# Weights split in one subtraction, and the operands of the last product split one stage earlier

## The chip, the cores and the metric

The kernel runs on one core of a Trainium2 chip. Its time is the device time of one execution in microseconds, the median of several; the profile is one more execution, recorded by the hardware.

## The reference

One encoder block on 512 tokens of width 2048, all in float32:

```
h = rmsnorm(x, norm1_w);  proj = h @ w_in                    # 2048 x 9248
group A, 8 heads: conv + silu, L2 norm, gated delta rule (chunks of 64), forward + backward scans
group B, 8 heads: HGRN2, f = lb + (1 - lb) * sigmoid(f_raw), k = 1 - f, forward + backward scans
x = x + concat(y_a, y_b) @ w_out                             # 2048 x 2048
h2 = rmsnorm(x, norm2_w)
x = x + (silu(h2 @ w_gate) * (h2 @ w_up)) @ w_down           # 2048 x 5632, twice, and 5632 x 2048
out = rmsnorm(x, norm_f_w)
```

## The kernel before

The kernel is written in a tile framework. A planner with a timeline model of the engines lays out the instructions of each engine in a fixed order; a stretch of code under `high_priority(offset=...)` is treated as if it stood that many instructions earlier in the program.

**The products.** Four large products stand one after the other, with the scans between the first and the second: the input projections (36 products of 256 output columns, `projections`, L313), the output product (8, `out_proj`, L866), gate and up (44, `gate_up`, L1028) and the last product, w_down (`down`, L1057). All go through `block_products` (L980), which computes products of 2 x 2 sub-matrices by seven multiplications in place of eight: the weights give seven operands of 128 x 128 (three sub-matrices and four sums), the activations seven of 128 x 256, and `PRODUCTS` (L930) says which meets which. Each operand is split into a high part, rounded to fp32r, and a low part, the rest, and each multiplication is three matmuls: high x high, high x low, low x high. A pair of row tiles is 7 x 3 = 21 matmuls of 256 columns.

**The weights.** `block_weights` (L957) prepares two such pairs at a time, a *block* of 42 matmuls. SyncE's queue loads two pieces of 256 KB into `raw` (three buffers). VectorE makes four sums in `wsum` (two buffers) with three operations (L972 to L974). Then for `raw` (128 x 768) and again for `wsum` (128 x 1024), ScalarE casts to `whi` and VectorE subtracts to `wlo` (L976, L977). `whi` and `wlo` have two buffers each, so a block is prepared while the one before it is multiplied. Where a group of operands has an odd number of pairs, its last block is half as large.

**The activations.** `operands` (L941) makes the seven operands of a pair: three VectorE operations for the sums (`act_sums`, L933), three ScalarE casts, three VectorE subtractions (L954), into slots `oh` and `ol`.

**After a product** `combine` (L1010) turns its four PSUM banks into the result: ScalarE copies one piece into a small tile, then VectorE does five operations (L1019 to L1023).

**Gate, up and the last product.** `gate_up` makes gate and up for 256 columns at a time (22 steps), multiplies them by the token scale (L1050), applies SiLU on ScalarE, multiplies the two (L1054), and stores the 512 KB result to DRAM through ScalarE's queue (L1055). `down` works in four groups of 6, 6, 5 and 5 operands (`DOWN_BLOCKS`, L1026), adding each group's product to an accumulator in SBUF. At the start of a group it loads each result from DRAM (L1070, ScalarE's queue) and splits it with `operands` into one of six slots. The slots of a group are free only when the last products of the group before have used them; the first two products of each group, and the last two of the first three groups, run together, block by block.

**Elsewhere.** In the projections' start (`activations`, L169) the transposed x is scaled by a column per partition on VectorE (L212). The forget gates get `lb + (1 - lb) * s` on VectorE (L389). `hgrn_pair` (L676) makes 1 - f for both directions on VectorE (L688, L689), in the scan stage.

Of the kernel before, what the change touches and what calls it, by code (L numbers as in the profile page):

```python
# [17 lines left out]
P = 128  # L18
T = 512
# [3 lines left out]
DFF = 5632  # L23
# [47 lines left out]
class Block:  # L71
# [97 lines left out]
    def activations(self, tops, acts, tmp):  # L169
# [24 lines left out]
        ops = []  # L194

        def chunk(i):
# [4 lines left out]
            for b in range(2):  # L201
                j = 2 * i + b
                full = tmp.tile([P, 2, T], F32, name=("t", "acc")[b], bufs=2)
                for r in range(2):
                    c = b + 2 * r
                    pt = bank(turn)
                    for t in range(NT):
# [11 lines left out]
                ts = tmp.tile([P, 4, ht], F32, name="comb", bufs=1) if b == 0 else \  # L219
                    tmp.tile([P, 2, T], F32, name="sq", bufs=1).rearrange("p a (b t) -> p (a b) t", b=2)  # L220
# [92 lines left out]
    def projections(self, xops, chunk, tmp):  # L313
# [62 lines left out]
        def post(kind, g, t):  # L376
# [30 lines left out]
        while n < len(self.AHEAD):  # L407
# [9 lines left out]
            for prod, (kind, g) in zip(prods, now):  # L417
                t = tmp.tile([P, 2, 2, ht], F32, name="t", bufs=2)
                self.combine(prod, t, tmp, 1, "comb")
# [256 lines left out]
    def hgrn_pair(self, h0):  # L676
# [11 lines left out]
        nc.vector.tensor_scalar(out=X[:, 0], in0=f[:, 0], scalar1=-1.0, scalar2=1.0, op0=ALU.mult, op1=ALU.add)  # L688
        nc.vector.tensor_scalar(out=X[:, 3], in0=f[:, 1], scalar1=-1.0, scalar2=1.0, op0=ALU.mult, op1=ALU.add)  # L689
# [107 lines left out]
    def mixers(self):  # L797
# [8 lines left out]
        self.wpairs, self.wbufs = 2, (3, 2, 2)  # L806
# [59 lines left out]
    def out_proj(self, late):  # L866
# [4 lines left out]
        def post(p, t):  # L871
# [4 lines left out]
            sq = late.tile([P, 2, T], F32, name="comb", bufs=1)  # L876
# [13 lines left out]
        for ps in ((0, 1), *((p,) for p in range(2, KT // 2))):  # L890
            k = [4 * (p // 2) + p % 2 for p in ps]
            prods = self.block_products([(a["w_out"][0], (i * P, (i + 2) * P)) for i in k], 0, yops, order=self.Y_BLOCKS)
            for p, prod in zip(ps, prods):
                t = late.tile([P, 2, 2, ht], F32, name="t", bufs=2)
                self.combine(prod, t, late, 1, "comb")
# [45 lines left out]
    def operands(self, ab, slot, sums, bufs):  # L941

        nc, ht = self.nc, self.HT
        pool = self.ops[slot // 2]
        h = pool.tile([P, 7, ht], F32R, name=f"oh{slot}")
        l = pool.tile([P, 7, ht], F32R, name=f"ol{slot}")
# [8 lines left out]
        return [h[:, i] for i in range(7)], [l[:, i] for i in range(7)]  # L955

    def block_weights(self, src, col):  # L957
# [6 lines left out]
        raw = cut(self.wst.tile([P, 4 * m, P], F32, name="raw", bufs=bufs[0]), 4)  # L964
        sm = cut(self.wst.tile([P, 4 * m, P], F32, name="wsum", bufs=bufs[1]), 4)
        h = cut(self.wst.tile([P, 7 * m, P], F32R, name="whi", bufs=bufs[2]), 7)
# [209 lines left out]
```

## Time and profile before

| | |
|---|---|
| runs | 2745.14, 2751.14, 2750.34 us; median 2750.34 |
| the profiled execution | 2746.68 us |
| its span | 2744.9 us |
| instructions | 55187 |
| mean granted TensorE clock | 0.963 of 2.4 GHz |
| moved by DMA | 361.89 MB, 132 GB/s on average |
| projections | about 15 to 900 us |
| scans | about 900 to 1140 us |
| output product and its operands | about 1140 to 1390 us |
| gate and up | about 1390 to 2245 us |
| last product | about 2245 to 2745 us |

Times in rows are microseconds from the span's start unless marked ns. PE is TensorE's matmuls, PEld its weight loads, DVE VectorE, ACT ScalarE, POOL GpSimd, SP SyncE; a `q` behind a name is that engine's queue of instructions that are not compute, DMA issues among them. `out<-in` gives tiles by their names in the program: `big` is a PSUM bank, `tsum`, `comb`, `u`, `yt`, `tt` are the tiles of `combine` and `operands`. A busy share of TensorE counts overlapping matmuls once, so the number of its instructions in a stretch says more about its pace. A few matmul records can be missing.

### The profile page before, as it was taken

Reading aid. Unit: us, or ns where it says so; the run is one execution under the profiler, and the core shown is the slowest. Engines: PE = TensorE matmul, PEld = TensorE weight load, DVE = VectorE, ACT = ScalarE, POOL = GpSimd, SP = SyncE. Lnnn points to the kernel's source line nnn. Section 1 sums busy time; section 2 is a strip of 40 time slices with the busy share of each in tenths; the row PEclk is TensorE's granted clock in tenths of the full one; section 3 lists DMA queues with packets and bytes.
Section 4 is the critical chain, followed back from the end, with each engine's and each line's share of the span. In section 5 each row is a group of like instructions: output and inputs, shape, how many; then the busy total and the mean of one; then the engine's idle time right before and its main releaser. Section 6 shows DMA issues by size and latency. Waiting matters only on the chain.

```text
span 2744.9 us, 55187 instructions
## 1 busy us (share of the span) xinstructions
PE 2520.9 (92%) x22511; PEld 2449.8 (89%) x22511; DVE 2506.7 (91%) x3978; ACT 1282.1 (47%) x1777; POOL 296.4 (11%) x148
## 2 busy tenths in 40 slices
PE   6999999888899587889999999999999999899996
PEld 5989999888899476789899999999999999898996
DVE  8999999998999887889998989999899999999996
ACT  6555655445454443444644434344433443444444
POOL 0121112223112554210000000000000000000000
PEclk9999999999999798999999999999999999999998
DMA  6334344556444643546434443434344364434333
GB/s 185 109 101 130 109 132 111 164 156 167 118 143 135 203 134 90 166 145 181 147 114 128 121 124 116 123 119 121 116 124 123 110 200 144 131 106 126 107 93 100
DMA packets 562345, 361.89 MB, mean 132 GB/s; under 512 B 51393, under 2 KB 514683, under 8 KB 562091
## 3 DMA queue, kind: packets, MB, share of 16 engines
q1 hardware_dynamic: 543515, 311.70, 39.6%
q10 hardware_dynamic: 18576, 46.67, 4.8%
q8 instruction: 176, 2.88, 0.4%
q14 instruction: 78, 0.64, 0.1%
HBM read 303.66 MB, written 54.62 MB: 131 GB/s over the span
## 4 chain that ended last, share of the span: by engine, by line
PE 49%; DVE 15%; issue 6%; DMA 4%; ACT 2%; POOL 1%; POOLq 0%; SPq 0%; ACTq 0%; DVEq 0%
PE big L1001 46%; DVE wlo L977 4%; DVE ol L954 1%; DVE wsum L972 1%; DVE wsum L974 1%; DMA L<-d_L 1%; DVE wsum L973 1%; ACT whi L976 1%; POOL acc L473 1%; DVE X L744 1%; DVE X L746 1%; DMA acc<-d_rows 0%; DVE lt L517 0%; DVE tsum L937 0%; PE oT L628 0%
## 5 line engine op out<-in xcount | busy, mean ns | idle before, releaser
L1001 PE MATMUL big<-oh,whi 128*128 128x256 f32 x4144 | 1139.1, 284 | 31.7 <-ACT whi L976 21.1
L1001 PE MATMUL big<-ol,whi 128*128 128x256 f32 x4144 | 1139.5, 282 | 1.8 <-DVE ol L954 1.6
L1001 PE MATMUL big<-oh,wlo 128*128 128x256 f32 x4144 | 1070.6, 283 | 16.8 <-DVE wlo L977 16.4
L1001 PEld LDWEIGHTS big<-oh,whi 128*128 128x128 f32 x4144 | 783.5, 190 | 42.4 <-ACT whi L976 28.8
L976 ACT CAST whi<-raw 128x768 fp32r<-128x768 f32 (+1 forms) x448 | 368.9, 824 | 907.3 <-PE big L1001 649.9
L1001 PEld LDWEIGHTS big<-ol,whi 128*128 128x128 f32 x4144 | 785.6, 190 | 3.3 <-DVE ol L954 2.8
L1001 PEld LDWEIGHTS big<-oh,wlo 128*128 128x128 f32 x4144 | 746.7, 190 | 22.6 <-DVE wlo L977 21.8
L977 DVE TENSOR_TENSOR wlo<-wsum,whi 128x1024 fp32r<-128x1024 f32 (+1 forms) x448 | 542.1, 1210 | 9.5 <-ACT whi L976 9.3
L976 ACT CAST whi<-wsum 128x1024 fp32r<-128x1024 f32 (+1 forms) x448 | 462.0, 1032 | 151.2 <-DVE wsum L974 148.1
L977 DVE TENSOR_TENSOR wlo<-raw,whi 128x768 fp32r<-128x768 f32 (+1 forms) x448 | 432.7, 966 | 85.9 <-ACT whi L976 82.2
L1001 PE MATMUL big<-tp,whi 128*128 128x256 f32 x2304 | 415.0, 286 | 27.9 <-ACT whi L976 17.0
L1001 PEld LDWEIGHTS big<-tp,whi 128*128 128x128 f32 x2304 | 348.5, 193 | 33.6 <-ACT whi L976 19.6
L972 DVE TENSOR_TENSOR wsum<-raw 128x512 f32<-128x512 f32 (+1 forms) x448 | 313.3, 700 | 10.2 <-DMA raw<-in_w_in 3.1
L1001 PE MATMUL big<-tp,wlo 128*128 128x256 f32 x1152 | 293.5, 290 | 21.7 <-DVE wlo L977 21.4
L1001 PE MATMUL big<-xh,whi 128*128 128x256 f32 x864 | 246.1, 289 | 10.4 <-ACT whi L976 7.3
L1001 PE MATMUL big<-xl,whi 128*128 128x256 f32 x864 | 244.8, 287 | 0.0
L1001 PE MATMUL big<-xh,wlo 128*128 128x256 f32 x864 | 229.3, 287 | 4.6 <-DVE wlo L977 4.3
L1001 PEld LDWEIGHTS big<-tp,wlo 128*128 128x128 f32 x1152 | 206.8, 195 | 28.8 <-DVE wlo L977 28.3
L974 DVE TENSOR_TENSOR wsum<-wsum,raw 128x256 f32<-128x256 f32 (+1 forms) x448 | 206.9, 463 | 2.4
L973 DVE TENSOR_TENSOR wsum<-wsum,raw 128x256 f32<-128x256 f32 (+1 forms) x448 | 189.4, 424 | 3.6
L1001 PEld LDWEIGHTS big<-xh,whi 128*128 128x128 f32 x864 | 167.7, 194 | 12.3 <-ACT whi L976 8.4
L1001 PEld LDWEIGHTS big<-xl,whi 128*128 128x128 f32 x864 | 166.7, 193 | 0.5
(302 smaller groups left out, 2628.2 us busy)
## 6 DMA issues: line engine op xcount, KB each, us to landing
raw<-in_w_in SPq DMA_DIRECT2D x288, 256.0 KB, 3.4
raw<-in_w_gate SPq DMA_DIRECT2D x176, 256.0 KB, 3.3
raw<-in_w_up SPq DMA_DIRECT2D x176, 256.0 KB, 3.4
raw<-in_w_down SPq DMA_DIRECT2D x160, 256.0 KB, 3.3
raw<-in_w_out SPq DMA_DIRECT2D x64, 256.0 KB, 4.2
d_t<-yt ACTq DMA_DIRECT2D x22, 512.0 KB, 4.1
tt<-d_t ACTq DMA_DIRECT2D x22, 512.0 KB, 4.0
d_x<-tp SPq DMA_DIRECT2D x16, 256.0 KB, 4.9
```

Source lines behind the costliest of these rows:

```text
L473: nc.gpsimd.tensor_tensor(out=gb, in0=gb, in1=gc, op=ALU.subtract)
L744: nc.vector.tensor_tensor(out=xv[:, 0:2, n, 0, :], in0=xv[:, 0:2, n, 0, :], in1=tv[:, :, n, 1:2].broadcast_to([P, 2, nb // 2, hs]), op=ALU ...
L746: nc.vector.tensor_tensor(out=xv[:, 2:4, n, 1, :], in0=xv[:, 2:4, n, 1, :], in1=tv[:, :, n, 0:1].broadcast_to([P, 2, nb // 2, hs]), op=ALU ...
L954: nc.vector.tensor_tensor(out=o, in0=src, in1=hh.bitcast(F32), op=ALU.subtract)
L972: tt(out=sm[:, 0:2], in0=raw[:, 0:1].broadcast_to([P, 2, n, P]), in1=raw[:, 2:0:-1], op=ALU.add)
L973: tt(out=sm[:, 2], in0=sm[:, 1], in1=raw[:, 2], op=ALU.add)
L974: tt(out=sm[:, 3], in0=sm[:, 2], in1=raw[:, 3], op=ALU.add)
L976: nc.scalar.copy(out=h[:, o], in_=src_)
L977: nc.vector.tensor_tensor(out=l[:, o], in0=src_, in1=h[:, o].bitcast(F32), op=ALU.subtract)
L1001: mm = lambda a, b, s, e: nc.tensor.matmul(prod[i], lhsT=a, rhs=b, start=s, stop=e, skip_group_check=True)
```

## The change

1. In `block_weights` parts and sums share one staging tile (`st`, 8 pieces, three buffers). The two casts stay, one per half; the low parts of all seven operands are made by one subtraction of 1792 columns after both casts.
2. `combine` takes four VectorE operations in place of five and no tile of its own; ScalarE's copy goes into a piece of the result.
3. `gate_up` splits each result itself and stores both parts (7 x 256 columns each, 7,168 bytes a row, 0.92 MB) to DRAM by two stores. `down` loads both into a slot by two loads under `high_priority`, with no computation. The second of gate_up's two result tiles has one buffer in place of two, and the pools for the loaded results are gone.
4. The scaling of x, the forget gates' affine and 1 - f move from VectorE to ScalarE.
5. Small tiles that were named `comb` use others (`sq`, `tsum`).

```
@@ activations, projections, hgrn_pair @@
-                    nc.vector.tensor_scalar(out=full[:, r].rearrange("p (t c) -> p t c", c=P), in0=xt,
-                                            scalar1=w1[:, 4 * i + c:4 * i + c + 1], scalar2=None, op0=ALU.mult)
+                    nc.scalar.activation(out=full[:, r].rearrange("p (t c) -> p t c", c=P), in_=xt, func=AF.Copy,
+                                         scale=w1[:, 4 * i + c:4 * i + c + 1])
...
-                    nc.vector.tensor_scalar(out=s[:, kk], in0=s[:, kk], scalar1=self.lb[:, 1, r:r + 1],
-                                            scalar2=self.lb[:, 0, r:r + 1], op0=ALU.mult, op1=ALU.add)
+                    nc.scalar.activation(out=s[:, kk], in_=s[:, kk], func=AF.Identity, scale=self.lb[:, 1, r:r + 1],
+                                         bias=self.lb[:, 0, r:r + 1])
...
-        nc.vector.tensor_scalar(out=X[:, 0], in0=f[:, 0], scalar1=-1.0, scalar2=1.0, op0=ALU.mult, op1=ALU.add)
-        nc.vector.tensor_scalar(out=X[:, 3], in0=f[:, 1], scalar1=-1.0, scalar2=1.0, op0=ALU.mult, op1=ALU.add)
+        nc.scalar.activation(out=X[:, 0], in_=f[:, 0], func=AF.Copy, scale=-1.0, bias=1.0)
+        nc.scalar.activation(out=X[:, 3], in_=f[:, 1], func=AF.Copy, scale=-1.0, bias=1.0)
@@ block_weights @@
-        raw = cut(self.wst.tile([P, 4 * m, P], F32, name="raw", bufs=bufs[0]), 4)
-        sm = cut(self.wst.tile([P, 4 * m, P], F32, name="wsum", bufs=bufs[1]), 4)
+        st = cut(self.wst.tile([P, 8 * m, P], F32, name="raw", bufs=bufs[0]), 8)
...
-            tt(out=sm[:, 0:2], in0=raw[:, 0:1].broadcast_to([P, 2, n, P]), in1=raw[:, 2:0:-1], op=ALU.add)
-            tt(out=sm[:, 2], in0=sm[:, 1], in1=raw[:, 2], op=ALU.add)
-            tt(out=sm[:, 3], in0=sm[:, 2], in1=raw[:, 3], op=ALU.add)
-            for o, src_ in ((slice(0, 3), raw[:, 1:]), (slice(3, 7), sm)):
-                nc.scalar.copy(out=h[:, o], in_=src_)
-                nc.vector.tensor_tensor(out=l[:, o], in0=src_, in1=h[:, o].bitcast(F32), op=ALU.subtract)
+            nc.scalar.copy(out=h[:, 0:3], in_=st[:, 1:4])
+            tt(out=st[:, 4:6], in0=st[:, 0:1].broadcast_to([P, 2, n, P]), in1=st[:, 2:0:-1], op=ALU.add)
+            tt(out=st[:, 6], in0=st[:, 5], in1=st[:, 2], op=ALU.add)
+            tt(out=st[:, 7], in0=st[:, 6], in1=st[:, 3], op=ALU.add)
+            nc.scalar.copy(out=h[:, 3:7], in_=st[:, 4:8])
+            tt(out=l, in0=st[:, 1:8], in1=h.bitcast(F32), op=ALU.subtract)
@@ combine @@
-        nc.scalar.copy(out=c, in_=b1[:, 0])
-        tt(out=t[:, 0], in0=b26, in1=two(c), op=ALU.add)
-        tt(out=c, in0=t[:, 0, 1], in1=b73[:, 0], op=ALU.add)
-        tt(out=t[:, 1], in0=b45, in1=two(c), op=ALU.subtract)
-        tt(out=t[:, 0, 1], in0=t[:, 0, 1], in1=b73[:, 1], op=ALU.add)
-        tt(out=t[:, 0, 1], in0=t[:, 0, 1], in1=b45[:, 1], op=ALU.subtract)
+        self.nc.scalar.copy(out=t[:, 1, 0], in_=b1[:, 0])
+        tt(out=t[:, 0], in0=b26, in1=two(t[:, 1, 0]), op=ALU.add)
+        tt(out=t[:, 1], in0=b73, in1=two(t[:, 0, 1]), op=ALU.add)
+        tt(out=t[:, 0, 1], in0=t[:, 1, 1], in1=b45[:, 1], op=ALU.subtract)
+        tt(out=t[:, 1, ::-1], in0=b45[:, ::-1], in1=two(t[:, 1, 0]), op=ALU.subtract)
@@ gate_up @@
-                t = (tb if i else self.io).tile([P, 2, 2, ht], F32, name=("yt", "u")[i], bufs=2)
+                t = (tb if i else self.io).tile([P, 2, 2, ht], F32, name=("yt", "u")[i], bufs=2 - i)
...
-            nc.scalar.dma_start(out=self.d_t[p], in_=g)
+            split = [tb.tile([P, 7, ht], F32R, name=f"d{n}") for n in "hl"]
+            self.split_operands(g, *split, self.io, 2)
+            for d, o in zip(self.d_t[p], split):
+                nc.scalar.dma_start(out=d, in_=o.bitcast(F32))
@@ down @@
-                tt = more.tile([P, 2, T], F32, name="tt", bufs=1) if bi and i % 3 == 2 else tio.tile([P, 2, T], F32, name="tt", bufs=2)
-                nc.scalar.dma_start(out=tt, in_=self.d_t[p0 + i])
                 with self.tc.high_priority(offset=2300):
-                    ops.append(self.operands(tt, (p0 + i) % 6, more if bi and i % 2 else tio, 1))
+                    hl = self.slot((p0 + i) % 6)
+                    for d, o in zip(self.d_t[p0 + i], hl):
+                        nc.scalar.dma_start(out=o.bitcast(F32), in_=d)
+                ops.append([[o[:, x] for x in range(7)] for o in hl])
```

`split_operands` is the body of `operands` with the slots handed in, and `slot` makes the slots' tiles.

## Rows read from the trace of the kernel before

**Rows 1.** The page's part 1, busy us of each engine, share of the span, instructions.

```profile
PE 2520.9 (92%) x22511; PEld 2449.8 (89%) x22511; DVE 2506.7 (91%) x3978; ACT 1282.1 (47%) x1777; POOL 296.4 (11%) x148
```

**Rows 2.** Busy time by stretch: stretch, length, engines' busy us (instructions), clock, DMA share, GB/s.

```profile
15.00:900.00 885.00, 811.32 (x6391) 787.59 (x6392) 836.18 (x1308) 480.68 (x606) 165.36 (x59) 0.96 0.48 136
...
1390.00:2245.00 855.00, 849.70 (x7131) 847.39 (x7132) 778.19 (x1162) 351.68 (x422) 0.00 (x0) 1.00 0.41 123
...
300.00:500.00 200.00, 188.67 (x1532) 185.26 (x1532) 194.09 (x275) 112.23 (x134) 30.88 (x13) 0.98 0.46 128
...
1600.00:1800.00 200.00, 200.00 (x1692) 200.00 (x1691) 180.46 (x267) 80.81 (x97) 0.00 (x0) 1.00 0.40 122
```

**Rows 3.** The same view, stretches of 30 us in the last product.

```profile
2215.00:2245.00 30.00, 26.16 (x184) 24.67 (x183) 29.58 (x52) 14.66 (x19) 0.00 (x0) 0.89 0.43 131
2245.00:2275.00 30.00, 28.89 (x238) 28.27 (x238) 29.44 (x47) 11.68 (x14) 0.00 (x0) 0.99 1.01 324
2305.00:2335.00 30.00, 30.00 (x258) 30.00 (x257) 28.77 (x46) 12.05 (x15) 0.00 (x0) 1.00 0.36 106
2350.00:2380.00 30.00, 20.76 (x140) 18.95 (x140) 30.00 (x51) 12.41 (x16) 0.00 (x0) 0.86 0.46 141
2485.00:2515.00 30.00, 24.11 (x173) 22.09 (x172) 30.00 (x52) 13.39 (x17) 0.00 (x0) 0.94 0.35 111
2590.00:2620.00 30.00, 25.06 (x182) 22.96 (x181) 30.00 (x54) 15.10 (x24) 0.00 (x0) 0.94 0.35 104
```

**Rows 4.** Timeline of VectorE in the gate and up stage: start, duration, instruction.

```profile
1710.51 0.96 DVE L977 TENSOR_TENSOR wlo<-raw,whi 128x768 fp32r<-128x768 f32 x1
1711.38 0.69 DVE L1021 TENSOR_TENSOR u<-big,comb 128x512 f32<-128x512 f32 x1
1711.98 0.41 DVE L1022 TENSOR_TENSOR u<-u,big 128x256 f32<-128x256 f32 x1
1712.31 1.22 DVE L977 TENSOR_TENSOR wlo<-wsum,whi 128x1024 fp32r<-128x1024 f32 x1
1713.45 0.41 DVE L1023 TENSOR_TENSOR u<-u,big 128x256 f32<-128x256 f32 x1
```

**Rows 5.** Groups of instructions by line and shape, VectorE: busy us, mean ns, idle before.

```profile
L977 DVE TENSOR_TENSOR wlo<-wsum,whi 128x1024 fp32r<-128x1024 f32 x432 | 531.2, 1230 | 9.1 <-ACT whi L976 8.9
L977 DVE TENSOR_TENSOR wlo<-raw,whi 128x768 fp32r<-128x768 f32 x432 | 423.9, 981 | 85.1 <-ACT whi L976 81.4 <-PE big L1001 0.4
...
L389 DVE TENSOR_SCALAR sig<-sig,lb 128x512 f32<-128x512 f32 x16 | 8.4, 562 | 1.5 <-ACT sig L322 1.4
...
L212 DVE TENSOR_SCALAR acc<-tp,w 128x512 f32<-128x512 f32 x8 | 3.7, 472 | 0.0
```

**Rows 6.** The same view, ScalarE.

```profile
L329 ACT ACTIVATE acc<-t,convw 128x512 f32<-128x512 f32 x24 | 16.2, 717 | 17.4 <-POOL t L421 17.4
```

**Rows 7.** The chain that ended last, in order of time: start, us, what.

```profile
1028.21 2.81 DVE X L688
```

**Rows 8.** Timeline of ScalarE in the gate and up stage.

```profile
1714.68 0.84 ACT L976 CAST whi<-raw 128x768 fp32r<-128x768 f32 x1 [3.26 <-PE big L1001]
1715.42 1.05 ACT L976 CAST whi<-wsum 128x1024 fp32r<-128x1024 f32 x1
```

**Rows 9.** Waits of ScalarE in the last product: us in total, times, longest.

```profile
ACT oh L952 <- PE big L1001: 13.6, 6, 3.7
```

**Rows 10.** Waits of TensorE in the projections.

```profile
PE big L1001 <- DVE wlo L977: 25.7, 32, 2.8
PE big L1001 <- ACT whi L976: 24.3, 13, 5.1
```

**Rows 11.** DMA issues in 2335 to 2350 us: count, KB each, us to landing.

```profile
raw<-in_w_down SPq DMA_DIRECT2D x6, 256.0 KB, 3.3
tt<-d_t ACTq DMA_DIRECT2D x3, 512.0 KB, 3.9
```

**Rows 12.** DMA issues in 2245 to 2260 us.

```profile
raw<-in_w_down SPq DMA_DIRECT2D x4, 256.0 KB, 6.6
```

More of the change, by code (lines that the diff above doesn't have):

```diff
@@ L218, in chunk @@
                     self.split_act(src, hi, lo)
-                ts = tmp.tile([P, 4, ht], F32, name="comb", bufs=1) if b == 0 else \
-                    tmp.tile([P, 2, T], F32, name="sq", bufs=1).rearrange("p a (b t) -> p (a b) t", b=2)
+                ts = tmp.tile([P, 2, T], F32, name="sq", bufs=1).rearrange("p a (b t) -> p (a b) t", b=2)
                 self.act_sums(ts, full)
@@ L875, in post @@
             nc.sync.dma_start(out=self.d_xt[p].rearrange("k p t -> p k t"), in_=t)
-            sq = late.tile([P, 2, T], F32, name="comb", bufs=1)
+            sq = self.io.tile([P, 4, ht], F32, name="tsum", bufs=2).rearrange("p (k h) t -> p k (h t)", k=2)
             nc.scalar.activation(out=sq, in_=t, func=AF.Square)
@@ L894, in out_proj @@
                 t = late.tile([P, 2, 2, ht], F32, name="t", bufs=2)
-                self.combine(prod, t, late, 1, "comb")
+                self.combine(prod, t)
                 last = t.rearrange("p n h t -> p n (h t)")
@@ L941, in operands, with slot, split_operands @@
     def operands(self, ab, slot, sums, bufs):
+        h, l = self.slot(slot)
+        self.split_operands(ab, h, l, sums, bufs)
+        return [h[:, i] for i in range(7)], [l[:, i] for i in range(7)]
+    def slot(self, slot):
+        return [self.ops[slot // 2].tile([P, 7, self.HT], F32R, name=f"o{n}{slot}") for n in "hl"]
+    def split_operands(self, ab, h, l, sums, bufs):
         nc, ht = self.nc, self.HT
-        pool = self.ops[slot // 2]
-        h = pool.tile([P, 7, ht], F32R, name=f"oh{slot}")
-        l = pool.tile([P, 7, ht], F32R, name=f"ol{slot}")
         ts = sums.tile([P, 4, ht], F32, name="tsum", bufs=bufs)
@@ L1008, in block_products, with combine @@
         return [banks for _, _, _, banks in todo]
[L1010 to L1012 removed]
+    def combine(self, prod, t):
         b26, b45, b73, b1 = prod
[L1014 to L1023 removed]
+        tt = self.nc.vector.tensor_tensor
+        two = lambda x: x.unsqueeze(1).broadcast_to([P, 2, self.HT])
+        self.nc.scalar.copy(out=t[:, 1, 0], in_=b1[:, 0])
[3 more added lines that the diff above has]
+        tt(out=t[:, 1, ::-1], in0=b45[:, ::-1], in1=two(t[:, 1, 0]), op=ALU.subtract)
     DOWN_BLOCKS = (6, 6, 5, 5)
@@ L1029, in gate_up @@
         nc, a, ht = self.nc, self.a, self.HT
-        self.d_t = [self.dram.tile([P, 2, T], F32, name=f"d_t{p}") for p in range(DFF // P // 2)]
+        self.d_t = [[self.dram.tile([P, 7, ht], F32, name=f"d_{n}{p}") for n in "hl"] for p in range(DFF // P // 2)]
         rb = self.rbc.unsqueeze(1).broadcast_to([P, 2, T])
@@ L1054, in gate_up, with down @@
             nc.vector.tensor_tensor(out=g, in0=g, in1=u, op=ALU.mult)
[L1055 to L1057 removed]
+            split = [tb.tile([P, 7, ht], F32R, name=f"d{n}") for n in "hl"]
+            self.split_operands(g, *split, self.io, 2)
+            for d, o in zip(self.d_t[p], split):
+                nc.scalar.dma_start(out=d, in_=o.bitcast(F32))
+    def down(self, ab_, tmp):
         nc, a, ht = self.nc, self.a, self.HT
@@ L1151, in run @@
                 token_scale = self.out_proj(pool("late", late))
-            tio = pool("tio", side="left")
             self.gate_up(token_scale, pool("tb", ffn))
-        self.down(tio, pool("more", side="left"), pool("accs"), pool("dtmp"))
+        self.down(pool("accs"), pool("dtmp"))
 TCKW = dict(schedule_with_timeline_sim=True)
```

23 lines of the change are left out of this document (8 added, 15 removed).

## The prediction

> **What bounds the kernel now.** I read the page first: TensorE is busy 92% of the span, VectorE 91%, ScalarE 47% [rows 1]. Two engines near full say nothing about which one sets the pace, so next came the busy time by stage. TensorE's busy time is flattering where matmuls trickle, so the reader should count its instructions. Where nothing holds TensorE, 1692 of them fit into 200 us, 118.2 ns each [rows 2]. Nearly the whole gate and up stage (1390 to 2245 us) runs at that pace, with VectorE busy 778.2 of 855 us: TensorE is the bound there. In the projection stage the pace is lower. In 300 to 500 us VectorE is busy 194.1 of 200 us and TensorE gets through 1532 instructions, 9.5% fewer; over 15 to 900 us VectorE is busy 836.2 of 885 us [rows 2]. There VectorE is close to being the bound. The last product shows both: a full 258 instructions per 30 us inside a block group, and 140 to 184 at the seams where the next group's operands are split, with VectorE at 29.6 to 30.0 of 30 us [rows 3].
>
> So a microsecond taken off VectorE is worth something in the projections and at the seams, and nothing in gate and up; a microsecond added to gate and up is free only while VectorE keeps up.
>
> **The change part by part.** Prices of VectorE come from start to start, since neighbouring instructions overlap in the records [rows 4]: 0.87 us for 768 columns, 0.60 for 512, 1.14 for 1024, 0.33 for 256. That is about 1.05 ns a column and 0.06 us an instruction.
>
> *Low parts in one operation.* Two subtractions (768 and 1024 columns, 2.01 us) become one of 1792: 1.14 + 768 x 1.055 ns = 1.95 us. That saves 0.06 us when VectorE runs back to back. By whole durations, 981 and 1230 ns [rows 5], the slope is 0.97 ns a column, the one operation 1.98 us and the saving 0.23 us. I take 0.1, nearer the first, as the engine mostly runs back to back. Of 448 blocks (432 of full size) 144 are in the projections, 32 in the output product, 176 in gate and up, 96 in the last product: 14, 3, 18 and 10 us of VectorE.
>
> *Four-operation combination.* Before: 0.60 + 0.33 + 0.60 + 0.33 + 0.33 = 2.19 us; after 3 x 0.60 + 0.33 = 2.13. 120 times 0.06 is 7 us: 2 in the projections, 3 in gate and up, 2 in the last product, under 1 in the output product.
>
> *VectorE to ScalarE.* The forget-gate affine, 16 x 0.56 us, and the scaling of x, 16 x 0.47 [rows 5], leave VectorE: 9 + 7.5 us less their overlap, say 15. On ScalarE each costs about 0.72 us (512 columns with a scale per partition) [rows 6], 23 us in a stage where it is busy 480.7 of 885 [rows 2]: hidden by its idle half, except in the first 60 us. The whole projection stage thus loses 14 + 2 + 15 = 31 us of VectorE work. It is not all worth time, since VectorE there also waits for others; the ends are 0 and 31, and I take two thirds, **-20 us**, because VectorE's share (94%) is nearest to that of a bound.
>
> *Two affine operations per HGRN pair in the scan.* Three of the eight stand on the chain that ended last, at about 2.8 us each [rows 7]. On ScalarE 1024 columns cost 1.05 us [rows 8], and its share of the whole span is 47% [rows 1]. Three times 1.7 is 5 us; the ends are 0 and 5 (other links may take over), I take **-4**. The output product: 3.5 us of VectorE, **-3**, ends 0 and -4.
>
> *Operands split ahead.* One split is 0.60 + 0.33 + 0.33 (sums) + 0.33 + 0.60 + 1.14 (lows) = 3.33 us of VectorE. 22 of them, 73 us, leave the last product and enter gate and up. There VectorE gets 73 - 18 - 3 = 52 us more: 830 of 855 us, 97.1%. TensorE ran full with VectorE at 28.77 of 30 us, 95.9% [rows 3], and lost 9.5% at 97.0% in the projections [rows 2]. So the ends are 0 and +90 us (855 x 1692/1532 - 855). I take what stands over 95.9%, 830 - 820 = **+10**, since the full-pace row comes from the same loop with no GpSimd beside it, as this stage is, and the other does not. ScalarE's extra 22 x 1.9 us of casts (1792 columns) fall on an engine busy 41% of this stage [rows 2]. Two stores of 0.92 MB instead of one of 0.52 issue from ScalarE's queue; the loop that reads them starts later, so nobody waits. SP's and GpSimd's queues get nothing new.
>
> At the four seams TensorE got through 184, 140, 173 and 182 instructions in 30 us against 258 [rows 3]: 353 missing at 0.116 us, 41 us, clock dips (0.86 to 0.94) included. With no split left there, VectorE drops by 73 + 12 us over the stage and ScalarE by 42. The ends are 0 and -41; I take 85%, **-35**, as nothing else is seen to be late at a seam.
>
> What is late next is the load. A slot now takes 1.84 MB instead of 0.5. At a seam of six operands a product is 6 x 21 x 118.2 ns = 14.9 us, and two products share each operand on both sides; so the slots come free from 22 us before the seam on, and are needed from the seam to 22 us after: 11.0 MB in 44 us, 250 GB/s, on top of 106 GB/s for weights. The queues moved 324 GB/s when full, 2245 to 2275 us, and TensorE still made 238 of 258 [rows 3]. So the last slot is 10% of 44 us late, 4 us, at one seam, and under 1 at the smaller ones: **+6**, ends 0 and the third rival's price. These loads wait on ScalarE's queue for a slot to come free, with weight casts behind them; the casts they replace waited there too, 13.6 us over 6 waits [rows 9], so I add nothing.
>
> *One buffer less between the two halves.* The merged operation starts only after the second cast. In gate and up a buffer comes free when TensorE ends a block; two casts (1.8 us from start to end [rows 8]) and 1.95 us later the lows are ready, while the next block runs 42 x 118.2 ns = 4.96 us. About 1.1 us of slack stays, where it was over 3. I cost it at nothing with that cover; the second rival is the case without. The staging tile shared by parts and sums lives longer, but there are three.
>
> The sum: -20 - 4 - 3 + 10 - 35 + 6 = -46 us. The profiled execution took 2746.7 us (its span 2744.9), so 2701; the median of the runs shown is 3.6 us above it, and I give **2704 us**.
>
> **The rivals.**
>
> *More of it arrives* (2669 us). The projections gain all 31 us, gate and up loses nothing, the seams close wholly: -31 - 5 - 4 - 41 = -81. For it: 97% is still under full, and clock dips go away along with stalls. Against: each term at its best end. Chance 0.17.
>
> *The merged low part stalls TensorE* (about 2740). Already in the projections TensorE waits 32 times, 25.7 us, for low parts, and 13 times, 24.3 us, for the casts [rows 10]. If each of the 32 waits grows by the 1.14 us that the first half no longer gains on the second, 36 us come back: -46 + 36 = -10. Against: the instructions are laid out anew by a planner that can put the high-part matmuls first. Chance 0.13.
>
> *The wide loads starve the weight loads* (about 2740). While three 0.5 MB operand loads ran on ScalarE's queue, weight loads still landed in 3.3 us [rows 11], which speaks against it; with the queues full they took 6.6 us [rows 12], which speaks for it. If the queues took turns row by row, a 7,168-byte row against one of 512, weights would get 22 of 324 GB/s instead of 106. Over the 34 us that 11 MB take, 2.9 MB would be missing, 5.5 blocks of 0.52 MB; staging covers two, so 3.5 blocks of 4.96 us, 17 us, and 12 at each smaller seam: 41 us in place of the 6 above, -11 in all. The Trainium skill's page DMA: Bandwidth & Descriptors, section on queues, rings and completion order, says that the engines take turns between queues packet by packet, not by bytes. By that rule the sum would be -11 instead of -46; rows 11 bear it out little. Chance 0.10.
>
> *Slower: VectorE becomes the bound of gate and up* (about 2784). The place is the steady loop at 1390 to 2245 us. Its VectorE share, 97.1%, is that of 300 to 500 us, where the pace was 9.5% lower [rows 2]: +90 in place of +10, in all +34. It decides the sign once that stage's pace falls by more than about 6.5% (56 us lost). For it: one engine runs its instructions in a fixed order, and a split's 1.14 us piece in front of a low part eats the whole slack. Against: the full pace at 95.9%. Chance 0.15.
>
> That the splits stay in the last product can't be: its loop issues loads only. The forecast itself has 0.45.
>
> **How the numbers follow.** A measurement of this kernel tells about 0.2%, 5.5 us, from no change. The forecast and the first rival (0.62) are faster; the two near 2740 give up 10 us at most to chance, so 0.13 of their 0.23 counts faster, 0.08 same, 0.02 slower; the last is slower: 0.75, 0.08, 0.17. The range, 2664 to 2752, holds the forecast with its terms' ends, the first three rivals, and leaves out the last and a little beyond the first.
>
> **What would show it.** Right: 258 instructions per 30 us through the seams; the operand casts and subtractions gone after the last gate and up product; gate and up within 10 us of its 855; VectorE's low parts 448 times at some 2 us; projections ending some 20 us sooner. Wrong: gate and up with gaps before matmuls that read low parts (last rival, or second in the projections); weight loads that land in over 10 us around a seam (third); ScalarE idle before a slot load with casts behind it. A loss in gate and up above 56 us would make the sign wrong.

## The result, and the profile after

The changed kernel takes 2835.36 us (median of 4 runs), the one before 2747.87 us beside it: ratio 1.0317, 95% interval 1.0299 to 1.0335. That is 87 us slower, where 46 us faster was predicted. (The tables give each kernel its name; the ones that begin with e are the experiments below.)

The trace gives five boundaries: the last matmul that reads `tp`, the first that reads `oh`, the first `combine` operation of gate, that of the last up product, and the final reduction. Lengths of the stages that they end, the first counted from the span's start, in us, here and in the runs that follow. The first seam, where the last product begins, lies on both sides of the boundary between gate and up and the last product:

| kernel | projections | scan | output product | gate and up | last product |
|---|---|---|---|---|---|
| before | 900.2 | 241.3 | 244.0 | 848.1 | 494.5 |
| after | 927.3 | 234.1 | 252.0 | 883.3 | 519.0 |
| e1_low | 922.6 | 239.6 | 255.6 | 846.9 | 516.9 |
| e2_split | 903.5 | 242.3 | 243.5 | 854.0 | 496.9 |
| e3_comb | 909.1 | 256.4 | 243.5 | 841.9 | 497.9 |
| e4_act | 904.9 | 235.2 | 244.0 | 847.6 | 495.9 |
| e5_stage | 907.6 | 259.9 | 258.8 | 863.1 | 501.9 |
| e6_narrow | 905.9 | 242.1 | 243.7 | 864.1 | 500.7 |
| e7_half | 904.4 | 235.5 | 244.8 | 852.4 | 489.9 |
| e8_twolow | 902.7 | 243.7 | 251.4 | 870.7 | 518.6 |
| e9_sep | 908.7 | 251.0 | 235.6 | 853.3 | 498.8 |
| e10_raw2 | 901.4 | 246.9 | 250.3 | 951.4 | 525.3 |
| e11_third | 899.7 | 235.4 | 244.6 | 850.1 | 482.1 |
| e12_nolow | 901.1 | 241.1 | 246.7 | 853.7 | 463.6 |
| e13_thirdall | 902.7 | 236.1 | 244.7 | 842.3 | 505.1 |
| e14_thirdcomb | 893.4 | 235.8 | 244.3 | 842.1 | 502.7 |
| e15_comb_third | 895.1 | 237.0 | 243.6 | 850.1 | 480.6 |

So 27 us come in the projections, 8 in the output product, 35 in gate and up and 24 in the last product; only the scan is shorter, by 7. Page of after, part 1 (answers to [rows 1]):

```profile
PE 2552.2 (90%) x22511; PEld 2477.7 (87%) x22511; DVE 2440.1 (86%) x3370; ACT 1306.3 (46%) x1817; POOL 261.6 (9%) x148
```

VectorE lost 67 us of work, as it should, and fell from 91% to 86%. The time went up all the same, so VectorE's load is not what grew. For the kernel after, busy time by stretch (columns as in [rows 2], [rows 3]):

```profile
15.00:900.00 885.00, 792.16 (x6200) 769.01 (x6200) 805.36 (x1076) 485.73 (x621) 133.10 (x54) 0.95 0.46 131
1600.00:1800.00 200.00, 195.25 (x1629) 193.18 (x1629) 180.10 (x235) 85.76 (x106) 0.00 (x0) 1.00 0.48 149
2250.00:2280.00 30.00, 23.24 (x166) 22.74 (x166) 12.08 (x13) 6.27 (x8) 0.00 (x0) 0.83 1.05 379
2280.00:2310.00 30.00, 21.24 (x124) 19.74 (x123) 23.31 (x34) 9.52 (x13) 0.00 (x0) 0.76 0.48 161
2400.00:2430.00 30.00, 20.94 (x176) 20.67 (x176) 14.19 (x16) 7.72 (x10) 0.00 (x0) 0.92 0.92 327
2550.00:2580.00 30.00, 21.14 (x156) 20.52 (x156) 18.43 (x26) 7.97 (x10) 0.00 (x0) 0.83 0.94 330
2670.00:2700.00 30.00, 20.82 (x143) 19.95 (x142) 16.94 (x23) 7.58 (x12) 0.00 (x0) 0.77 0.85 309
```

In the projections VectorE is 31 us less busy than in [rows 2] and TensorE does 191 instructions fewer. In gate and up 1629 instead of 1692 fit into 200 us, with VectorE at 90%, as before. The seams are as deep as before (124 to 176 of 258), but now VectorE stands idle for 22 to 60% of them, and in four of the five the DMA engines are 85% busy or more. What each waits for in after (waits: us in total, times, longest), first TensorE in 15 to 930 us, answering to [rows 10]:

```profile
PE big L1003 <- DVE wlo L979: 61.4, 44, 4.3
PE big L1003 <- ACT whi L974: 9.7, 7, 3.4
```

then VectorE in gate and up (1415 to 2295 us); before, that list had no wait for a weight load:

```profile
DVE raw L975 <- DMA raw<-in_w_gate: 36.1, 35, 2.4
DVE raw L975 <- DMA raw<-in_w_up: 23.7, 17, 9.5
DVE wlo L979 <- ACT whi L978: 21.6, 25, 3.4
```

Two new signs, then: TensorE waits for low parts more than twice as long as before (61.4 us against 25.7; its waits for casts fell from 24.3 to 9.7, so the two together grew by 21), and VectorE, which runs in a fixed order, stands before sums whose weights haven't landed.

### The profile page after: what moved, and what is told of

The parts are those of the page before. It is cut to its first block, busy times and chain, and to the rows that moved or that the text cites. A ratio compares the mean times of both kernels' runs of the same rounds, so it can differ in the third digit from the quotient of the medians.

```text
span 2832.6 us, 54723 instructions
## 1 busy us (share of the span) xinstructions
PE 2552.2 (90%) x22511; PEld 2477.7 (87%) x22511; DVE 2440.1 (86%) x3370; ACT 1306.3 (46%) x1817; POOL 261.6 (9%) x148
## 5 line engine op out<-in xcount | busy, mean ns | idle before, releaser
L1003 PE MATMUL big<-oh,wlo 128*128 128x256 f32 x4144 | 1038.5, 285 | 42.6 <-DVE wlo L979 42.5
L979 DVE TENSOR_TENSOR wlo<-raw,whi 128x1792 fp32r<-128x1792 f32 (+1 forms) x448 | 908.9, 2029 | 86.4 <-ACT whi L978 83.4
L1003 PEld LDWEIGHTS big<-oh,wlo 128*128 128x128 f32 x4144 | 733.0, 192 | 55.3 <-DVE wlo L979 54.4
L978 ACT CAST whi<-raw 128x1024 fp32r<-128x1024 f32 (+1 forms) x448 | 461.2, 1030 | 72.7 <-DVE raw L977 58.2
L975 DVE TENSOR_TENSOR raw<-raw 128x512 f32<-128x512 f32 (+1 forms) x448 | 326.6, 729 | 181.5 <-DMA raw<-in_w_in 56.7
L1003 PE MATMUL big<-tp,whi 128*128 128x256 f32 x2304 | 429.0, 286 | 12.3 <-DVE ld L481 6.6
L1003 PE MATMUL big<-tp,wlo 128*128 128x256 f32 x1152 | 308.8, 287 | 0.0
L1003 PE MATMUL big<-xh,wlo 128*128 128x256 f32 x864 | 235.7, 299 | 61.7 <-DVE wlo L979 61.4
L1003 PE MATMUL big<-xh,whi 128*128 128x256 f32 x864 | 244.8, 290 | 9.8 <-ACT whi L974 9.7
L1003 PE MATMUL big<-xl,whi 128*128 128x256 f32 x864 | 242.3, 287 | 0.6 <-DVE xl L82 0.6
L1003 PEld LDWEIGHTS big<-xh,wlo 128*128 128x128 f32 x864 | 159.5, 197 | 72.9 <-DVE wlo L979 72.0
L1003 PEld LDWEIGHTS big<-tp,wlo 128*128 128x128 f32 x1152 | 216.5, 196 | 0.2
L977 DVE TENSOR_TENSOR raw<-raw 128x256 f32<-128x256 f32 (+1 forms) x448 | 203.7, 456 | 3.3
L976 DVE TENSOR_TENSOR raw<-raw 128x256 f32<-128x256 f32 (+1 forms) x448 | 195.1, 436 | 2.6
```

The costliest lines, as they stand in the source:

```text
L975: tt(out=st[:, 4:6], in0=st[:, 0:1].broadcast_to([P, 2, n, P]), in1=st[:, 2:0:-1], op=ALU.add)
L976: tt(out=st[:, 6], in0=st[:, 5], in1=st[:, 2], op=ALU.add)
L977: tt(out=st[:, 7], in0=st[:, 6], in1=st[:, 3], op=ALU.add)
L978: nc.scalar.copy(out=h[:, 3:7], in_=st[:, 4:8])
L979: tt(out=l, in0=st[:, 1:8], in1=h.bitcast(F32), op=ALU.subtract)
L1003: mm = lambda a, b, s, e: nc.tensor.matmul(prod[i], lhsT=a, rhs=b, start=s, stop=e, skip_group_check=True)
```

## The experiments

**One part at a time.** e1_low takes over the shared tile, the one subtraction and the combination; e2_split only the splitting ahead; e3_comb only the combination; e4_act only the moves to ScalarE. e1_low and later e5_stage need room and so have one `u` and two `tt` buffers.

> The kernel before with the shared staging tile, the one subtraction for all low parts and the four-operation combination; splits stay in the last product, nothing moves to ScalarE (to make room the up result has one buffer and the loaded results two in place of three). Theory, that the merged low part comes too late for TensorE: most of the lost time in the projections and in gate and up is here already, projections end near 920 us in place of 900, gate and up takes some 870 in place of 848, total 2780 to 2800 us. Rival, that gate and up lost its time to the splits' extra VectorE work: gate and up stays at 848, total 2735 to 2750.

> The kernel before with only the operands of the last product split ahead and loaded through DRAM. Theory, that the wide loads starve the weight loads at the seams: the last product takes 510 to 520 us in place of 494, weight loads around a seam land in 10 us and over; gate and up, with two subtractions per block, keeps its pace to within 10 us; total 2765 to 2785. Rival, that VectorE's extra work makes gate and up slower: gate and up at 880, total above 2790. If neither holds, the seams close and the total is 2705 to 2720.

> The kernel before with only the four-operation combination. Theory, that it saves 0.06 us of VectorE 120 times and costs nothing: 2740 to 2748 us. Rival, that its longer chain (every operation needs the one before) holds PSUM banks longer: TensorE waits on banks, 2755 and over.

> The kernel before with only the operations that move from VectorE to ScalarE. Theory, that they relieve VectorE in the projections: projections end 5 to 15 us sooner, total 2730 to 2745. Rival, that ScalarE's casts queue behind them: projections end 5 to 15 us later, total 2755 to 2765, with longer waits of TensorE on casts.

Ratios to before: e1_low 1.0188 [1.0163, 1.0213], e2_split 1.0036 [1.0022, 1.0050], e3_comb 1.0059 [1.0044, 1.0074], e4_act 0.9971 [0.9960, 0.9982]. The weights' preparation is the large loss; splitting ahead, meant to bring most, is no gain; only the moves to ScalarE help, by 0.3%.

The stages fit the expectations less well than the totals do. e1_low ends where its theory's range does (2800.56 us) and loses in the projections (922.6), as the theory has it, and in the output and last products (12 and 22 us), but gate and up stays at 846.9, which was the rival's sign: the merging and the tile don't make up that stage's loss by themselves. e2_split meets none of its three ranges: its last product takes 496.9 us, neither 510 to 520 nor a closed seam's time. e3_comb's total is in its rival's range, but its loss lies in the scan (+15 us), whose instructions it doesn't touch, and the projections (+9); more on that at the end. e4_act's total is in its theory's range for another reason than the theory's: the projections end 4.7 us later, though VectorE is 19 us less busy in them (817.59 us against 836.18 [rows 2]), and the scan is 6 us shorter.

```profile
15.00:900.00 885.00, 811.35 (x6351) 785.32 (x6352) 817.59 (x1272) 496.32 (x635) 171.70 (x55) 0.96 0.47 134
```

**The subtraction and the tile, apart.** e5_stage is e1_low, and e8_twolow is after, with

```
-            tt(out=l, in0=st[:, 1:8], in1=h.bitcast(F32), op=ALU.subtract)
+            tt(out=l[:, 0:3], in0=st[:, 1:4], in1=h[:, 0:3].bitcast(F32), op=ALU.subtract)
+            tt(out=l[:, 3:7], in0=st[:, 4:8], in1=h[:, 3:7].bitcast(F32), op=ALU.subtract)
```

> The kernel of e1_low with its one subtraction for all low parts put back as two (768 and 1024 columns), still in the shared staging tile, both casts and both loads as there. Theory, that the one subtraction comes too late for TensorE: the projections end near 909 us, as with the four-operation combination alone, TensorE's wait for low parts in them falls from 60 to under 35 us, total 2765 to 2775. Rival, that the shared tile is held too long and the next weights are loaded late: nothing comes back, projections end near 922, VectorE's wait for weight loads stays at about 50 us, total 2790 to 2805.

> The changed kernel with only the one subtraction put back as two in the shared staging tile. Theory, that gate and up lost its 35 us because the one subtraction left TensorE no slack once VectorE also splits: gate and up takes 850 to 860 us in place of 883, the projections 905 to 912, total 2775 to 2790. Rival, that VectorE's work alone did it: gate and up stays above 875, total 2810 and over.

e5_stage 1.0236 [1.0216, 1.0256], e8_twolow 1.0192 [1.0173, 1.0211]. In both pairs the projections are shorter with two subtractions: by 15.0 us (e1_low to e5_stage) and 24.6 us (after to e8_twolow). TensorE's waits there say why. e8_twolow, 15 to 900 us:

```profile
PE big L1004 <- DVE wlo L980: 32.9, 33, 2.6
PE big L1004 <- DVE wlo L979: 12.8, 12, 2.1
...
PE big L1004 <- ACT whi L974: 5.1, 5, 2.1
...
PE big L1004 <- ACT whi L978: 1.7, 2, 1.1
```

45.7 us, against 61.4 with one; with those for casts it is 52.5 us, near the 50.0 of before [rows 10], where after has 71.1. The two kernels with one subtraction, at 922.6 and 927.3 us, also lie outside the 893 to 909 us that the projections take in every other kernel of the table. In total the two pairs differ: after is 34 us slower than e8_twolow, but e1_low 12 us faster than e5_stage, where the merging goes with a shorter scan (20 us) and gate and up (16) and a longer last product (15). What is common to both is the loss in the projections. The totals on record fit neither side: e5_stage is slower than both its ranges and e8_twolow's gate and up, 870.7, lies between its two.

Two subtractions leave most of the loss. e5_stage, against e3_comb (both have the combination; the weight block and the buffers for room differ), loses 15 us in the output product and 21 in gate and up. It has the shorter projections of its theory and the waits for loads of its rival. Its row of 1600 to 1800 us:

```profile
1600.00:1800.00 200.00, 196.62 (x1648) 194.79 (x1647) 172.30 (x250) 78.70 (x93) 0.00 (x0) 1.00 0.40 118
```

VectorE is less busy than before (172.3 us against 180.5; neither kernel splits ahead) and TensorE still slower (1648 against 1692): no engine is full. VectorE's waits in gate and up of e5_stage (1400 to 2260 us):

```profile
DVE raw L971 <- DMA raw<-in_w_gate: 49.3, 54, 2.8
DVE raw L971 <- DMA raw<-in_w_up: 48.3, 52, 3.2
```

**The tile alone, from both sides.** e9_sep is after with the weight block of before: three tiles of parts, two of sums, each cast followed by its subtraction. e10_raw2 is before with one tile less from the output product on and no other edit:

```
-        self.wpairs, self.wbufs = 2, (3, 2, 2)
+        self.wpairs, self.wbufs = 2, (2, 2, 2)
         self.wst = pool("wst")
```

> The changed kernel with the weight block of the kernel before put back (three tiles of parts, two of sums, two casts each followed by its subtraction); splitting ahead, the four-operation combination and the moves to ScalarE stay. Theory (the shared staging tile is held until the low part is made, so weight loads are issued later and VectorE, which runs in a fixed order, waits for their landings): VectorE's waits for weight loads in gate and up fall from 50 us to under 15, gate and up takes 850 to 858 us instead of 883, the output product 244 to 247 instead of 252, the last product about 497 instead of 519, the projections 900 to 909 instead of 927; in all 2750 to 2768 us. Rival (gate and up is long because VectorE is too full there once the splits have moved in, whatever the tiles): VectorE has 24 us more work in that stage with two subtractions, so gate and up stays at 880 us or grows, and the total stays above 2790.

> The kernel before with two instead of three tiles for the loaded parts from the output product on; no instruction is changed. If lookahead of the loads is what the shared tile takes away, this kernel has the same signs without any other part of the change: VectorE waits for weight loads in gate and up (nothing before) for tens of us, the output product grows by 8 us or more, gate and up by 15 us or more, the last product by 5 us or more; in all 2775 us or more. If two tiles are enough (the loads land in about 3 us of a block's 5), it stays within 5 us of before, and the shared tile costs through something else.

e9_sep took 2763.88 us, 1.0042 [1.0027, 1.0058]; e10_raw2 2893.82 us, 1.0512 [1.0490, 1.0534]. Both came as the theory of the tile has it, in the total and in gate and up; e10_raw2's output product grew by 6 us, not the 8 or more expected, and e9_sep's scan was 10 us longer and its output product 8 shorter than before's, which no theory had. e9_sep, by stretch:

```profile
1400.00:2245.00 845.00, 834.74 (x7017) 833.64 (x7016) 786.56 (x1186) 384.96 (x459) 0.00 (x0) 0.99 0.51 163
1600.00:1800.00 200.00, 200.00 (x1692) 200.00 (x1691) 189.79 (x288) 93.47 (x112) 0.00 (x0) 1.00 0.48 152
```

TensorE runs at the full 1692 with more VectorE work than in after (189.8 of 200 us): VectorE is not the bound there, and one `u` buffer, which e9_sep keeps, is not to blame. VectorE's waits for weight loads in the stage fall to 14.3 us in 3. In e10_raw2 the waits appear with no part of the change present; its VectorE waits over the whole span, and the stretch:

```profile
DVE wsum L972 <- DMA raw<-in_w_gate: 127.6, 78, 3.7
DVE wsum L972 <- DMA raw<-in_w_up: 65.3, 61, 2.7
```

```profile
1600.00:1800.00 200.00, 188.92 (x1509) 180.75 (x1508) 155.62 (x238) 75.80 (x86) 0.00 (x0) 1.00 0.36 106
```

e9_sep and e8_twolow differ in the tile and in one thing more: in e8_twolow both casts stand before the first subtraction, in e9_sep each cast is followed by its own. No run takes these apart; both bear on how long a tile is held.

How little it takes shows when each block's load, sums and low part are paired in the trace. VectorE's timeline of after (start, us; the brackets are idle time before) has one tile from its sums to its release:

```profile
1702.98 0.69 DVE L975 TENSOR_TENSOR raw<-raw 128x512 f32<-128x512 f32 x1 [1.16 <-DMA raw<-in_w_gate]
...
1710.73 2.02 DVE L979 TENSOR_TENSOR wlo<-raw,whi 128x1792 fp32r<-128x1792 f32 x1
```

The subtraction between them, at 1705.79, belongs to the tile before. Over the blocks of 1450 to 2200 us (134 to 151 in each kernel), medians in us, a block's first load being the first of its two, and the subtraction being the last that reads the loaded tile:

| kernel | first load issued to sums | sums to that subtraction | its start to the tile's next load |
|---|---|---|---|
| before | 6.7 | 7.2 | 0.99 |
| after | 4.9 | 8.0 | 2.05 |
| e1_low | 4.9 | 8.0 | 2.05 |
| e8_twolow | 4.9 | 8.9 | 1.25 |
| e5_stage | 4.2 | 9.1 | 1.25 |
| e10_raw2 | 4.0 | 6.0 | 0.98 |
| e9_sep | 8.7 | 4.9 | 0.98 |

(For e10_raw2 the next load is that of two blocks on, for the others of three.) Each next load follows at once on the last instruction that reads the tile: the 768-column subtraction before, the 1792-column one after, the second of two in e8_twolow and e5_stage. Three tiles turn over in about three blocks, 3 x 4.96 = 14.9 us, so what the tile is held longer is taken from the load: 6.7 us from issue to use become 4.9 or 4.2. The second piece is issued 0.4 us after the first and loads land 3.4 us after issue, so at about 4 us nothing is left. In e10_raw2 that state is reached with the old code.

With 4.9 us one microsecond is left, and e1_low shows that this can be enough. It has the same medians as after, and in gate and up it runs at full pace; VectorE waits 9.2 us there (1420 to 2260 us) for weight loads, against 59.8 in after:

```profile
1600.00:1800.00 200.00, 200.00 (x1692) 200.00 (x1691) 174.53 (x216) 80.47 (x96) 0.00 (x0) 1.00 0.40 119
```

```profile
DVE raw L971 <- DMA raw<-in_w_up: 6.5, 8, 2.3
DVE raw L971 <- DMA raw<-in_w_gate: 2.7, 6, 0.8
```

What after and e8_twolow have beside it in this stage are the splits and their stores (149 and 151 GB/s in 1600 to 1800 us in place of 119). So at 4.9 us the loss in gate and up needs both: a load that is issued late, and work or traffic that uses up the rest. Whether that is the splits' work or the stores, no run tells. At e5_stage's 4.2 us the stage loses without either.

**The seams.** e6_narrow is e2_split with the DRAM tiles laid out so that a row is 1,024 bytes instead of 7,168:

```
-self.dram.tile([P, 7, ht], F32, name=f"d_{n}{p}")
+self.dram.tile([7, P, ht], F32, name=f"d_{n}{p}").rearrange("x p t -> p x t")
```

e12_nolow is e2_split with the loads of `ol` left out after the first group, so the last product uses the first group's low parts in the later three.

> The kernel of e2_split with the same bytes stored and loaded in rows of 1,024 bytes in place of 7,168 (the seven operands lie apart in DRAM). Theory, that the queues take turns row by row, so that wide rows starve the weights' rows of 512 bytes: weight loads around the seams land in under 10 us (20.9 at most with wide rows), the seams lose a third to a half less, last product 475 to 488 us in place of 497, total 2735 to 2752. Rival, that the sum of the bytes is what the seams wait for: last product 495 to 505, total 2757 to 2770.

> The kernel with only the operands split ahead; after the first group the loads of the low parts are left out (each slot keeps those of the first group, so the low parts of three quarters of the last product's operands are others), which halves the bytes at the seams and adds no instruction. Theory (the bytes are what the seams wait for): the half-size loads land in about 5 us instead of 9, the seams nearly close, and the last product takes 470 to 482 us instead of 496.9. Rival (the wait is for the slots to come free and for the order in which ScalarE's queue issues, not for bytes): the last product stays within 5 us of 496.9.

e6_narrow 1.0075 [1.0055, 1.0095]; e12_nolow 0.9906 [0.9883, 0.9929]. DMA issues around the first seam (count, KB each, median us to landing), e2_split at 2220 to 2235 us:

```profile
oh<-d_h ACTq DMA_DIRECT2D x2, 896.0 KB, 8.7
...
raw<-in_w_down SPq DMA_DIRECT2D x2, 256.0 KB, 11.3
```

and e6_narrow at 2222 to 2242 us:

```profile
oh<-d_h ACTq DMA_DIRECT2D x2, 896.0 KB, 12.6
raw<-in_w_down SPq DMA_DIRECT2D x4, 256.0 KB, 8.0
```

With short rows the weights land sooner and the operands later, and the last product takes 500.7 us, not less; gate and up, with the first seam at its end, is 10 us longer. e6_narrow's total is in its rival's range. The Trainium skill's page DMA: Bandwidth & Descriptors, section on queues, rings and completion order, has the engines take turns between queues by packets; the trade agrees with that, and it buys no time: the seam needs both. Halving the bytes does. The second seam, e2_split:

```profile
2363.00:2393.00 30.00, 23.21 (x173) 22.01 (x172) 21.24 (x33) 8.12 (x12) 0.00 (x0) 0.89 0.89 308
```

and e12_nolow:

```profile
2363.00:2393.00 30.00, 30.00 (x257) 30.00 (x257) 27.73 (x43) 11.83 (x15) 0.00 (x0) 1.00 0.65 211
```

257 of 258, and so at the third seam; the last product, 463.6 us, is shorter than its expectation had it, by 33 us than e2_split's and by 31 than before's. The loads of `oh` still wait on ScalarE's queue for their slots, so these seams don't wait for slots to come free: they wait for what is loaded, whose bytes (and number of loads) are halved here. At the first seam, where both parts are still loaded, TensorE gets through 175 instructions in 2215 to 2245 us, as in e2_split (176).

That first seam stands at the end of gate and up. e9_sep, whose steady loop runs at full pace, loses there what it loses in that stage, with its loads filling the queues; its last 49 us of the stage, then before's:

```profile
2200.00:2249.00 49.00, 39.89 (x302) 39.20 (x301) 30.80 (x44) 13.93 (x18) 0.00 (x0) 0.90 0.96 348
```

```profile
2185.00:2234.00 49.00, 47.06 (x380) 45.89 (x380) 47.86 (x78) 25.68 (x36) 0.00 (x0) 0.98 0.55 169
```

**Sharing the work between VectorE and the queues.** e7_half has the moves to ScalarE, the whole first group and every second later operand split ahead; e11_third every third; e13_thirdall every third in the first group too; e14_thirdcomb and e15_comb_third are e13_thirdall and e11_third with the combination.

```
+        self.ahead = [i % 3 == 1 or bi == 0 for bi, nb in enumerate(self.DOWN_BLOCKS) for i in range(nb)]
...
+            if self.ahead[p]:
```

> The kernel of e2_split where in the last three groups only every second operand is split ahead and the others are split at the seam, plus the operations moved to ScalarE of e4_act. Theory, that a seam is bound by the loads when all are split ahead and by VectorE when none is: both halves hide beside each other, the last product takes 470 to 482 us, total 2725 to 2740, below the kernel before. Rival, that a seam costs what it costs in either way (clock dips, banks): last product 494 to 500, total 2745 to 2755.

> Before with the moves to ScalarE, all operands of the first group and two in each of the later groups split ahead (one in three instead of one in two). If at a seam the loaded bytes and VectorE's splits share the work, the seams gain from fewer bytes or lose from more splits: the last product lands between 488 and 494 us (one in two: 489.9; none: 494.5), and gate and up, with 4 splits fewer, gains up to 4 us on 852.4; in all 2733 to 2742 us. If it is under 2735 the best mix is nearer to few.

> As the run with one operand in three split ahead, but in the first group too (there all six were split ahead). Theory (at a seam the loads of operands split ahead and VectorE's splits must share the work): the first seam, where all runs that load all six show 190 to 200 of 258 TensorE instructions in its worst 30 us at 380 to 400 GB/s, gets 215 or more, and the end of gate and up with the last product shortens by 3 to 8 us; in all 2722 to 2729 us against 2731. If the first seam is bound by something else (weight loads of the first blocks of a new tensor), it stays at 2731 within 2 us.

> The run with one operand in three split ahead in every group, with the four-operation combination added. What it tells apart: alone on the kernel before, the combination cost 16 us, of which 15 lay in the scan, which it doesn't touch. If that was the layout of the plan and no cost of the combination, it comes out here within 6 us of the run without it, on either side, and its scan may be long or short; if the combination itself costs (the copy into the result's own tile holds it from the first product on), the projections grow by 5 to 10 us and the total by over 8 again.

> The run with the first group and one in three later operands split ahead, with the four-operation combination added. On the version without a whole first group the combination gained 9 us, all in the projections; alone on the kernel before it cost 16. If it is worth its 7 us of VectorE and the rest is the layout of the plan, this run lies within 9 us below and 5 us above 2731 and no scan or projection stage leaves the band of the runs so far (projections 893 to 909, scan 234 to 260); if it costs by itself on this base, it is above 2740.

| kernel | us | ratio to before |
|---|---|---|
| e7_half | 2738.62 | 0.9963 [0.9951, 0.9975] |
| e11_third | 2731.10 | 0.9922 [0.9905, 0.9940] |
| e13_thirdall | 2744.55 | 0.9980 [0.9970, 0.9991] |
| e14_thirdcomb | 2735.12 | 0.9936 [0.9923, 0.9950] |
| e15_comb_third | 2725.51 | 0.9929 [0.9915, 0.9942] |

e11_third at the second seam:

```profile
2350.00:2380.00 30.00, 26.72 (x207) 24.70 (x206) 30.00 (x51) 14.14 (x18) 0.00 (x0) 1.00 0.57 185
```

207 instructions where before had 140 [rows 3], at 185 GB/s and with VectorE full: the two now share it. The gain, 482.1 us, was larger than expected, and e7_half's (489.9) smaller. The two kernels differ by little: e7_half splits 13 of 22 operands ahead and e11_third 12, three against two of the second group's six; in the groups of five both split two. So what sets them apart is one operand fewer, not the four that the expectation counts, and which operands are split. e13_thirdall missed: TensorE stands still once, at the first seam.

```profile
PE big L1005 <- ACT oh L957: 26.3, 1, 26.3
```

Its chain of waits there:

```profile
2237.82 1.05 ACT dh L957
...
2238.89 5.33 DMA d_h<-dh
...
2244.30 4.26 DMA tt<-d_u
...
2249.03 1.10 PE big L1005 x3
```

The loads of what is still to be split stand behind the last split ahead and its store; so whether the first seam is bound by bytes too stays open. The combination gave -9.4 us on e13_thirdall (all in the projections), -5.6 on e11_third and +18 alone. On e11_third the ratios of the two kernels, with and without it, can't be told apart, and alone most of its loss was in the scan: no cost of its own is seen. (For e13_thirdall a change of at most 6 us was expected.) The scan, with the same operations throughout, lies between 234 and 260 us, as the planner lays the instructions out anew in each kernel; the projections, without the shared tile, between 893 and 909.

## Why the prediction was wrong

By medians, each against its own runs of before, the loss divides so: e9_sep (all but the weight block) +12 us, the shared tile with its order of casts (e8_twolow) another 41, the merging (after) another 34. The last two sizes hold in this order and with the splits ahead; without them the merging gained 12 us in total (e5_stage to e1_low).

- **Low parts, the staging tile** ("lives longer, but there are three", at nothing): this is the step that failed most. The tile is held until the low part is made, and the next load starts that much later: 4.9 us from issue to use in place of 8.7 (e9_sep to e8_twolow). It costs about 40 us: 16 in the output product, 17 in gate and up, 20 in the last product, less 7 in the scan and 6 in the projections. No rival had it.
- **Low parts, the merged operation** ("About 1.1 us of slack stays", at nothing; second rival +36): the second rival was right for the projections, where it costs 15 to 25 us by the waits that it named, though the saving on VectorE was there: 2064 ns for 1792 columns against 981 + 1230.
- **Projections, -20**: came as +27. With VectorE relieved and the old weight block they are no shorter than before's 900.2: 908.7 in e9_sep, 904.9 in e4_act, both inside the 893 to 909 by which layouts move them. VectorE's 94% did not make it the bound; the merging's loss there goes with when a low part comes, not with how full the engine is.
- **Scan, -4**: -7 in after, -6 in e4_act; the sign was right, but other layouts move this stage by more. **Output product, -3**: +8, the tile.
- **Gate and up, +10**: +35, but +6 in e2_split and +5 in e9_sep, so the +10 is near in size, and the rest is the tile and the merging. That is in part luck: the term was for a VectorE too full in the steady loop, and e9_sep runs that loop at full pace and loses at the first seam, to its loads. The fourth rival has the stage and the sign right and the cause wrong: e5_stage is slow there with VectorE at 86%, e9_sep full with VectorE at 95%. VectorE's share was overrated as well: 97.1% forecast, 93.1% in e9_sep (786.56 of 845 us).
- **Seams -35, loads +6**: together +2 in e2_split's last product, and the part of the first seam that lies in gate and up comes on top. The -35 is what e12_nolow gives (-31) once half the bytes are gone. The failed term is the load's: 250 GB/s over 44 us assumed that slots come free evenly; the trace has 300 to 380 GB/s for 30 us at each seam. The third rival was near in size (-35 and its 41 make +6), but not in its mechanism: e6_narrow lets the weights land sooner and saves nothing, so the bytes cost the time, not the turns between the queues. Its -11 in all came from the other terms.
- **ScalarE's share**, at nothing: no cost clear of the layouts; e4_act is 0.3% faster in all, with projections 4.7 us longer.

## What to carry to other kernels

A tile that is held one step longer costs lookahead (the time between the issue of a load and its use), and here lookahead was worth more than engine time, as VectorE runs its instructions in a fixed order: work out, before merging two tiles or two operations, how long a buffer is held and when its next load is due. Work moved off a full engine into DRAM becomes bytes at the moment when a buffer comes free; where both sides are near full, a mix (here the whole first group and two operands of each later one) gave a shorter last product than either end, by 12 to 15 us. And read an expected gain from a stall by what else is full in that stall.

## What was not expected of the hardware

VectorE's busy share is not a sum of prices. e2_split puts 29 more VectorE instructions into 200 us of gate and up, about 5 splits at 3.33 us from start to start, 17 us; the busy time rose from 180.46 us [rows 2] by under 9:

```profile
1600.00:1800.00 200.00, 199.57 (x1678) 198.66 (x1677) 189.20 (x296) 90.95 (x110) 0.00 (x0) 1.00 0.49 152
```

Neighbours overlap in the records [rows 4], so instructions that stood alone with whole durations can take less once others stand beside them; that this is the whole difference is not shown. And an engine with 10% idle time or more can be where the pace is lost, when it stands before loads in a fixed order: VectorE in after is busy 180.1 of 200 us, as in before (180.46), and in e5_stage 172.3.
